# Delta-rule layer: decay exponentials in one piece behind the first keys' Silus, the keys' inverse square by reciprocal, powers of the queries behind the solve

## The chip, the cores and the metric

The kernel runs on one core of a Trainium2 chip. The metric is the device time of one execution in microseconds (us), given as the median of several runs. TensorE is called PE here, VectorE DVE, ScalarE ACT, GpSimd POOL and SyncE SP.

## What is computed

The program is a decoder trunk of four layers over 256 tokens of width 1024: a pooling mixer, a gated delta-rule mixer, a latent attention mixer, and a pooling mixer again. All of the change lies in the second layer, apart from one constant that an earlier layer sets up. Cut to what matters, that layer computes (8 heads, keys and queries of 128 channels, values of 256):

```
def l2norm(x):
    return x * rsqrt(sum(x * x, -1) + EPS)

qkv, gate, b_raw, a_raw = split(h @ w_in)
q, k, v = split(silu(causal_depthwise_conv(qkv, conv_w)))     # 4 taps
q = l2norm(q) * 128 ** -0.5;  k = l2norm(k)
beta = sigmoid(b_raw)
g = -exp(a_log) * softplus(a_raw + dt_bias)
# per chunk of tokens and head:
g = cumsum(g);  decay[i, j] = exp(g[i] - g[j]) for j <= i, else 0
L = strict_lower((k * beta) @ k.T * decay)
u, w = solve(I + L, [v * beta, k * beta * exp(g)])
attn = (q @ k.T) * decay
v_new = u - w @ state
o = (q * exp(g)) @ state + attn @ v_new
state = state * exp(g_last) + (k * exp(g_last - g)).T @ v_new
o = rmsnorm(o) * silu(gate);  y = o @ w_out
```

## The kernel before

**Strips.** Each weight matrix is read in strips of 512 columns. A strip comes in four DMAs on SP's queue, of two blocks of 128 rows each, into one of three raw buffers. Each block is split in two parts (`weights`, L126): ACT casts the high part (`whi`, L149), DVE (or POOL for a few blocks) subtracts it to get the low part (`wlo`, L150), and three matmuls make up one product (`mm3`). The split parts lie in a ring of nine. A gate strip (`g0` to `g3`) has tokens in the rows of its result; strips of keys, queries and values (`k`, `q`, `v`) have channels there.

**The layer's steps.** Behind the strip of a `k` or `q` step, `channels` (L791) does this: ACT scales the strip's PSUM results by the first tap (`conv`, L755), DVE adds the three other taps (L758), ACT takes the Silu (L804), PE transposes (L810), ACT squares the transposed block (L813), and DVE sums the squares into `ssq` (L814). For keys, ACT also copies the transposed first half into `ktok` (L816). `keys` (L838) makes the factors of the heads of one half: `rk`, the inverse root of the sum, as a power on POOL (L789), and `s2 = rk * beta * rk` on DVE. `lower` (L848) has PE multiply keys with keys (`against`, L818) and DVE multiply that by `s2` and by the decays `DT` into `LT` (L832); the diagonal blocks are copied out by POOL (L858) and ACT (L856).

**The solve.** `substitution` (L860) transposes the blocks on DVE (L861) and solves them by 62 small multiplications and subtractions on POOL, one after another (L867, L871). `blocks_back` (L876) transposes the result back on DVE (L878) and copies it into `T`, half on ACT (L885) and half on POOL (L887). `inverses` (L943) joins the blocks by matmuls between the next strips. `queries` (L893) multiplies keys with queries, and sets the powers `rq` and `rq2` of the queries' sums on POOL (L904, L789, L907, L908), which only the layer's last steps read. `ktok` is multiplied by a decay on POOL (L888); the steps of the state read it (`state`, L1027).

**Decays.** The cumulative sums `G` come from a small matmul; they go through DRAM and come back spread over all partitions as `Gb` (L733). DVE subtracts and masks (`DT`, L740, 16 instructions), and `decays` (L745) exponentiates both `DT`, `Gb[1]` and `G` itself (`eG`) on ACT (L748). Silu and Exp use different tables of ACT; a switch shows in the trace as ACT_TABLE_LOAD under the line of the next activation.

**What sets the order.** The steps are emitted in the order of a list written by hand:

```
order = "g0 k0 d a0 k1 a1 s g1 q0 v0 v1 v2 b q1 i V3 c3 g2 u0 u1 g3".split()
```

Here `a` is `lower`, `d` the decays, `s` the substitution, `b` `blocks_back`, `i` the inverses, and `u` the news of the values. The framework gets the program with `schedule_with_timeline_sim=True` (L1422): it fixes at build time, by a timeline of its own, in which order each engine executes what was emitted, and may take a later instruction first when an earlier one isn't ready on that timeline. In the trace, for instance, PE runs the whole strip of `k1` before the transposes of `k0`. On the chip each engine then works through its queue in that fixed order, and an instruction that waits holds up all behind it. `later(x)` (L82) forces the instructions emitted under it to come after instruction `x` on the engine of `x`; `mark` keeps the last instruction of several kinds: `mark["conv"]` the last tap, `mark["gate"]` the last Silu of a gate strip, `mark["blocks"]` the last step of the substitution, `mark["strip"]` the last matmul of a strip with channels in the rows.

Of the kernel before, what the change touches and what calls it, by code (L numbers as in the profile page):

```python
# [16 lines left out]
P = 128  # L17
# [7 lines left out]
EPS = 1e-6  # L25
# [17 lines left out]
def trunk(ctx: ExitStack, tc: tile.TileContext, x, positions, norm_g, pool_w_in, pool_w_grp,  # L43
# [466 lines left out]
    def pool_layer(i, j, hT):  # L510
# [80 lines left out]
        for g in order:  # L591
            gs = gate(g)
            if not place:
                with later(*[m for k, m in mark.items() if k not in ("rest", "strip", "conv")]):
                    turn_params()
                    window_counts()
            elif setups:
                with later(*[m for k, m in mark.items() if k not in ("rest", "strip", "conv")]):
                    setups.pop(0)()
            pT = pooled(g)  # L600
            if waiting:
                mixed(*waiting)
            waiting = (g, pT, gs)
# [8 lines left out]
    def gdn_setup():  # L612
# [11 lines left out]
        for a in range(2):  # L624
            nc.gpsimd.memset(m32[64 * a + 32:64 * a + 64, a], 1.0)
        half = const.tile([P, NT, GDN_H // 2], F32, name="halves")
        nc.gpsimd.memset(half, -0.5)
        cols = workb("cols", 2, 32)
# [28 lines left out]
    def gdn_layer(i, j, hT):  # L657
# [22 lines left out]

        order = "g0 k0 d a0 k1 a1 s g1 q0 v0 v1 v2 b q1 i V3 c3 g2 u0 u1 g3".split()
        while order[0][0] == "g":
# [38 lines left out]
        nc.vector.tensor_copy(flat(G), ps[:, :M])  # L721
        Gf, lf = flat(G), flat(lga)


# [12 lines left out]
        DT = [big("DT", H, P) for _ in range(NT)]  # L737
        for t in range(NT):
            for h in range(H):
                nc.vector.scalar_tensor_tensor(out=DT[t][:, h, :], in0=Gb[t][:, h, :],  # L740
                                               scalar=G[:, t, h:h + 1], in1=maskT,
                                               op0=ALU.subtract, op1=ALU.min)
        Eb = Gb[1]

        def decays():  # L745
            with later(*[m for n, m in mark.items() if n == "gate"]):
                for a in (*DT, Eb, eG):
                    nc.scalar.activation(a, G if a is eG else a, AF.Exp)  # L748

# [28 lines left out]
        for t in range(NT):  # L778
# [4 lines left out]
        ssq = small("ssq", 2, NT, H, bufs=1)  # L783
        rk, rki, rq, rq2, s1, s2 = (
            sc(n) for n in ("rk", "rki", "rq", "rq2", "s1", "s2"))
        neG = small("neG", H, bufs=1)

        def power(o, a):
            nc.gpsimd.tensor_tensor(out=o, in0=a, in1=half, op=ALU.pow)  # L789

        def channels(dst, c0, hf, which):  # L791
# [4 lines left out]
            for b in range(2):  # L796
                cv = [worka("cv", S) for _ in range(2)]
                conv(*[(banks[b][:, c * S:(c + 1) * S], (c0 + hf * CW) // P + 2 * b + c, cv[c])
                       for c in range(2)])
                for c in range(2):  # L800
                    o, v = dst[hf][:, 2 * b + c, :], cv[c]
                    if which:
                        o, v = halves(o), parted(v)
                    nc.scalar.activation(o, v, AF.Silu)  # L804
            for c in range(0, 4, 2):
# [32 lines left out]
        def keys(hf):  # L838
            hs = slice(4 * hf, 4 * hf + 4)
            channels(kT, GDN_QK, hf, 0)  # L840
            nc.gpsimd.tensor_scalar(ssq[:, 0, :, hs], ssq[:, 0, :, hs], EPS, None, ALU.add)
            power(rk[:, :, hs], ssq[:, 0, :, hs])
            nc.vector.tensor_tensor(out=s1[:, :, hs], in0=rk[:, :, hs], in1=beta[:, :, hs],
                                    op=ALU.mult)
            nc.vector.tensor_tensor(out=s2[:, :, hs], in0=s1[:, :, hs], in1=rk[:, :, hs],
                                    op=ALU.mult)

# [12 lines left out]
        def substitution():  # L860
# [3 lines left out]
            for r in range(B - 1):  # L864
# [7 lines left out]
                                                         op=ALU.subtract).ins  # L872
            nc.vector.reciprocal(rki, rk)
            nc.vector.tensor_scalar(neG, eG[:, 1, :], -1.0, None, ALU.mult)

        def blocks_back():  # L876
# [4 lines left out]
            for d in range(Q):  # L881
# [4 lines left out]
                else:  # L886
                    nc.gpsimd.tensor_copy(o, tv[dd])  # L887
            nc.gpsimd.tensor_tensor(out=ktok, in0=ktok, op=ALU.mult,  # L888
                                    in1=DT[0][:, :, P - 1:].to_broadcast([P, H, P]))

        at_ = []

        def queries(hf):  # L893
# [5 lines left out]
            ev = Eb[:, 4 * hf:4 * hf + 4, :]  # L899
            rh, qh = rq[:, :, 4 * hf:4 * hf + 4], rq2[:, :, 4 * hf:4 * hf + 4]  # L900

            nc.vector.tensor_tensor(out=ev, in0=ev, in1=qT[hf][:, :, P:], op=ALU.mult)
            with later(mark["blocks"]):
                nc.gpsimd.tensor_scalar(qh, ssq[:, 1, :, 4 * hf:4 * hf + 4], float(P), EPS * P,  # L904
                                        ALU.mult, ALU.add)
                power(rh, qh)
                nc.gpsimd.tensor_tensor(out=qh, in0=rh, in1=rh, op=ALU.mult)  # L907
                nc.gpsimd.tensor_scalar(qh, qh, 1.0 / DV, None, ALU.mult)  # L908

# [84 lines left out]
        def news(hf):  # L994
# [3 lines left out]
            for b in range(2):  # L998
# [6 lines left out]
                for c in range(2):  # L1005
# [5 lines left out]
                 "c": values_done}  # L1011
        once = {"s": substitution, "d": decays, "b": blocks_back, "i": inverses}
        for name in order:
# [419 lines left out]
```

## Time and profile before

| what | value |
|---|---|
| median of 3 runs | 816.21 us (813.97 to 816.85) |
| profiled execution | 817.07 us |
| its span, first to last instruction | 815.4 us |
| granted PE clock, mean | 0.992 |
| busy: PE, DVE, ACT, POOL | 794.6, 598.6, 500.2, 148.7 us |
| HBM read | 136.74 MB |

Rows of a timeline give the start, the duration, the engine, the line, the operation, output<-inputs, and how many instructions were merged; brackets hold the idle time of the engine ahead of the row and what ended it. Rows of a window give its bounds and length, the busy time of PE, PE's weight loads, DVE, ACT and POOL, the granted clock, and the DMA's share and rate. Matmul ends are modelled, so a busy PE says only that it had work. In this execution the delta-rule layer's strips run from about 170 to 340 us of the span.

### The profile page before, as it was taken

The numbers are of one execution on the slowest core, as the hardware profiler recorded it, in microseconds if no ns is written. First come the engines' busy times: TensorE is split into PE (matmuls) and PEld (weight loads), VectorE is DVE, ScalarE is ACT, GpSimd is POOL, SyncE is SP. The second block draws the span as 40 slices with busy tenths as digits, with TensorE's granted clock in tenths as the row PEclk, the third lists the DMA queues.
The fourth block names the chain that finished last, engine by engine and source line by source line (L and its number), as shares of the span: only waits on it lengthen the run. The fifth ranks groups of instructions, "written<-read, shape, count | busy, mean of one in ns | idle before, by whom it ended". The sixth has DMA issues, their size and how long they took to land.

```text
span 815.4 us, 16122 instructions
## 1 busy us (share of the span) xinstructions
PE 794.6 (97%) x5966; PEld 754.8 (93%) x5966; DVE 598.6 (73%) x1133; ACT 500.2 (61%) x1009; POOL 148.7 (18%) x292
## 2 busy tenths in 40 slices
PE   8989999999989989999999999999999999999996
PEld 7979999989889988888989999999999989999996
DVE  4699987667889976456677659778877667877863
ACT  6566555567876855455565654566655575566662
POOL 3001100233037852022212013000000210000011
PEclk9999999999999999999999999999999999999999
DMA  6765666746455633323557686753652646676562
GB/s 208 227 177 177 197 214 219 219 154 209 152 161 156 205 113 100 127 73 108 182 148 221 204 191 183 208 145 87 182 172 74 187 153 196 191 222 207 198 213 53
DMA packets 106615, 138.85 MB, mean 170 GB/s; under 512 B 19044, under 2 KB 48936, under 8 KB 106536
## 3 DMA queue, kind: packets, MB, share of 16 engines
q1 hardware_dynamic: 104032, 136.07, 55.2%
q0 software_dynamic: 320, 1.06, 0.4%
q8 instruction: 47, 0.77, 0.4%
q10 hardware_dynamic: 2184, 0.69, 0.4%
q14 instruction: 32, 0.26, 0.1%
HBM read 136.74 MB, written 1.06 MB: 169 GB/s over the span
## 4 chain that ended last, share of the span: by engine, by line
PE 85%; POOL 5%; ACT 3%; DVE 3%; issue 2%; DMA 1%; ACTq 0%; SPq 0%; DVEq 0%; POOLq 0%
PE acc L162 69%; PE aux L162 8%; POOL X L867 2%; POOL U L871 2%; ACT whi L149 1%; PE tp L1337 1%; DVE cv L758 1%; DMA x<-in_x_dram 1%; DVE wlo L150 1%; PE aux L823 1%; ACT junk L256 1%; PE tp L419 0%; PE aux L979 0%; PE aux L961 0%; PE aux L1002 0%
## 5 line engine op out<-in xcount | busy, mean ns | idle before, releaser
L150 DVE TENSOR_TENSOR wlo<-raw,whi 128x512 fp32r<-128x512 f32 (+1 forms) x370 | 250.1, 702 | 98.4 <-ACT whi L149 96.1
L149 ACT CAST whi<-raw 128x512 fp32r<-128x512 f32 (+1 forms) x380 | 223.1, 618 | 156.1 <-PE acc L162 78.9
L162 PE MATMUL acc<-hTl,whi 128*128 128x256 f32 x832 | 230.5, 277 | 0.0
L162 PE MATMUL acc<-hTh,whi 128*128 128x256 f32 x832 | 229.3, 276 | 0.0
L162 PE MATMUL acc<-hTh,wlo 128*128 128x256 f32 x832 | 229.1, 276 | 0.0
L162 PEld LDWEIGHTS acc<-hTl,whi 128*128 128x128 f32 x832 | 160.1, 192 | 0.2
L162 PEld LDWEIGHTS acc<-hTh,whi 128*128 128x128 f32 x832 | 160.0, 192 | 0.3
L162 PEld LDWEIGHTS acc<-hTh,wlo 128*128 128x128 f32 x832 | 159.9, 192 | 0.1
L162 PE MATMUL acc<-wlo,yTh 128*128 128x256 f32 (+1 forms) x384 | 112.3, 311 | 0.0
L162 PE MATMUL acc<-whi,yTh 128*128 128x256 f32 (+1 forms) x384 | 112.3, 315 | 0.0
L162 PE MATMUL acc<-whi,yTl 128*128 128x256 f32 (+1 forms) x384 | 89.1, 313 | 0.0
L162 PEld LDWEIGHTS acc<-wlo,yTh 128*128 128x128 f32 x384 | 73.2, 191 | 3.1
L162 PEld LDWEIGHTS acc<-whi,yTh 128*128 128x128 f32 x384 | 72.9, 191 | 3.1
L162 PEld LDWEIGHTS acc<-whi,yTl 128*128 128x128 f32 x384 | 63.1, 191 | 3.4
L153 ACT ACTIVATE whi<-raw,gain 128x512 fp32r<-128x512 f32 x64 | 43.7, 719 | 31.1 <-DMA raw<-in_pool_w_in_dram 25.6
L153 ACT ACTIVATE whi<-raw,colsT 128x512 fp32r<-128x512 f32 x64 | 44.5, 722 | 29.5 <-DMA raw<-in_pool_w_out_dram 18.1
L154 DVE SCALAR_TENSOR_TENSOR wlo<-raw,colsT,whi 128x512 fp32r<-128x512 f32 x64 | 47.4, 762 | 19.0 <-ACT whi L153 18.4
L162 PE MATMUL acc<-wlo,hTh 128*128 128x512 f32 (+1 forms) x144 | 54.1, 381 | 0.4 <-DVE wlo L150 0.2
L154 DVE SCALAR_TENSOR_TENSOR wlo<-raw,gain,whi 128x512 fp32r<-128x512 f32 x64 | 46.2, 743 | 10.0 <-ACT whi L153 7.5
L162 PE MATMUL acc<-whi,hTh 128*128 128x512 f32 (+1 forms) x144 | 52.8, 379 | 0.7 <-ACT hTh L242 0.7
L387 POOL TENSOR_TENSOR hg<-x,gain 128x256 f32<-128x256 f32 x16 | 13.4, 846 | 208.3 <-DVE x L451 208.3
L162 PE MATMUL acc<-whi,hTl 128*128 128x512 f32 (+1 forms) x144 | 42.5, 373 | 0.0
(368 smaller groups left out, 1526.2 us busy)
## 6 DMA issues: line engine op xcount, KB each, us to landing
raw<-in_pool_w_in_dram SPq DMA_DIRECT2D x62, 512.0 KB, 4.6
raw<-in_gdn_w_in_dram SPq DMA_DIRECT2D x48, 512.0 KB, 3.9
raw<-in_pool_w_out_dram SPq DMA_DIRECT2D x32, 512.0 KB, 4.6
raw<-in_mla_w_in_dram SPq DMA_DIRECT2D x24, 512.0 KB, 4.5
raw<-in_mla_w_uq_dram SPq DMA_DIRECT2D x36, 256.0 KB, 3.6
raw<-in_pool_w_grp_dram SPq DMA_DIRECT2D x16, 512.0 KB, 3.8
raw<-in_gdn_w_out_dram SPq DMA_DIRECT2D x16, 512.0 KB, 3.5
raw<-in_mla_w_ukv_dram SPq DMA_DIRECT2D x32, 256.0 KB, 3.4
```

The lines of the kernel that those rows point to most:

```text
L149: a = nc.scalar.copy(hi, v)
L150: b = e.tensor_tensor(out=lo, in0=v, in1=hi.bitcast(F32), op=ALU.subtract)
L153: a = nc.scalar.activation(hi, v, AF.Copy, scale=g)
L154: b = e.scalar_tensor_tensor(out=lo, in0=v, scalar=g, in1=hi.bitcast(F32), op0=ALU.mult, op1=ALU.subtract)
L162: return nc.tensor.matmul(inorder(o, n), lhsT=lhs, rhs=woven(rhs, n), start=start, stop=stop)
L256: nc.scalar.activation(junk[:, :n], src, AF.Square, scale=scale, accum_out=o)
L387: nc.gpsimd.tensor_tensor(out=self.early[t, a], in0=xs[t][:, sl], in1=self.g[:, sl], op=ALU.mult)
L758: mark["conv"] = nc.vector.scalar_tensor_tensor(out=o[:, d:], in0=ps[:, :S - d], scalar=tp(3 - d, c), in1=o[:, d:], op0=ALU.mult, op1=ALU. ...
L823: nc.tensor.matmul(ps[:, b], lhsT=kT[hf][:, b, tt], rhs=rhs[hf][:, b, tt], start=True, stop=True)
L867: nc.gpsimd.tensor_tensor(out=pv, op=ALU.mult, in0=Lb[:, r + 1:, r:r + 1].to_broadcast([P, n, c]), in1=Tb[:, r:r + 1, :c].to_broadcast([P, ...
L871: mark["blocks"] = nc.gpsimd.tensor_tensor(out=tv, in0=tv, in1=pv, op=ALU.subtract).ins
L1337: nc.tensor.transpose(ps[:, a * P:(a + 1) * P], sb[:, a * P:(a + 1) * P], ident)
```

## The change

Five things in the one layer:

1. `decays` no longer waits for the gate's Silu. It now holds the 16 subtractions of DVE too, and everything in it comes after the first keys' last tap on DVE (`mark["conv"]`) and after their last Silu on ACT (`mark["silu"]`, which is new). The exponential of `G` is emitted where `G` is made.
2. The keys' factor is `s2 = beta / (ssq + EPS)`, by a reciprocal and a multiplication on DVE. `rki`, which was the reciprocal of `rk`, is now the root of the sum, as a power of 0.5 on POOL.
3. The queries' powers leave `queries` for a step of their own, `query_norms` (`n`), behind `i`. Its instructions on POOL come after the last POOL copy of `blocks_back`.
4. The multiplication of `ktok` by the decay moves to the end of that step.
5. The list of steps has `q0` ahead of `g1`, and `n` behind `i`.

```
-        half = const.tile([P, NT, GDN_H // 2], F32, name="halves")
-        nc.gpsimd.memset(half, -0.5)
+        half = const.tile([P, 2, NT, GDN_H // 2], F32, name="halves")
+        for a in range(2):
+            nc.gpsimd.memset(half[:, a], a - 0.5)
...
-        order = "g0 k0 d a0 k1 a1 s g1 q0 v0 v1 v2 b q1 i V3 c3 g2 u0 u1 g3".split()
+        order = "g0 k0 d a0 k1 a1 s q0 g1 v0 v1 v2 b q1 i n V3 c3 g2 u0 u1 g3".split()
...
-        Gf, lf = flat(G), flat(lga)
+        Gf = flat(G)
+        nc.scalar.activation(eG, G, AF.Exp)
...
-        for t in range(NT):
-            for h in range(H):
-                nc.vector.scalar_tensor_tensor(out=DT[t][:, h, :], in0=Gb[t][:, h, :],
-                                               scalar=G[:, t, h:h + 1], in1=maskT,
-                                               op0=ALU.subtract, op1=ALU.min)
...
         def decays():
-            with later(*[m for n, m in mark.items() if n == "gate"]):
-                for a in (*DT, Eb, eG):
-                    nc.scalar.activation(a, G if a is eG else a, AF.Exp)
+            with later(mark["conv"], mark["silu"]):
+                for t in range(NT):
+                    for h in range(H):
+                        nc.vector.scalar_tensor_tensor(out=DT[t][:, h, :], in0=Gb[t][:, h, :],
+                                                       scalar=G[:, t, h:h + 1], in1=maskT,
+                                                       op0=ALU.subtract, op1=ALU.min)
+                for a in (*DT, Eb):
+                    nc.scalar.activation(a, a, AF.Exp)
...
-                    nc.scalar.activation(o, v, AF.Silu)
+                    mark["silu"] = nc.scalar.activation(o, v, AF.Silu).ins
...
-            nc.gpsimd.tensor_scalar(ssq[:, 0, :, hs], ssq[:, 0, :, hs], EPS, None, ALU.add)
-            power(rk[:, :, hs], ssq[:, 0, :, hs])
-            nc.vector.tensor_tensor(out=s1[:, :, hs], in0=rk[:, :, hs], in1=beta[:, :, hs],
-                                    op=ALU.mult)
-            nc.vector.tensor_tensor(out=s2[:, :, hs], in0=s1[:, :, hs], in1=rk[:, :, hs],
-                                    op=ALU.mult)
+            n, r = ssq[:, 0, :, hs], s2[:, :, hs]
+            nc.vector.tensor_scalar(n, n, EPS, None, ALU.add)
+            nc.vector.reciprocal(r, n)
+            nc.vector.tensor_tensor(out=r, in0=r, in1=beta[:, :, hs], op=ALU.mult)
+            nc.gpsimd.tensor_tensor(out=rki[:, :, hs], in0=n, in1=half[:, 1], op=ALU.pow)
...
-            nc.vector.reciprocal(rki, rk)
...
-                    nc.gpsimd.tensor_copy(o, tv[dd])
-            nc.gpsimd.tensor_tensor(out=ktok, in0=ktok, op=ALU.mult,
-                                    in1=DT[0][:, :, P - 1:].to_broadcast([P, H, P]))
+                    mark["back"] = nc.gpsimd.tensor_copy(o, tv[dd]).ins
...
-            with later(mark["blocks"]):
-                nc.gpsimd.tensor_scalar(qh, ssq[:, 1, :, 4 * hf:4 * hf + 4], float(P), EPS * P,
-                                        ALU.mult, ALU.add)
-                power(rh, qh)
-                nc.gpsimd.tensor_tensor(out=qh, in0=rh, in1=rh, op=ALU.mult)
-                nc.gpsimd.tensor_scalar(qh, qh, 1.0 / DV, None, ALU.mult)
+
+        def query_norms():
+            with later(mark["back"]):
+                nc.gpsimd.tensor_scalar(rq2, ssq[:, 1], float(P), EPS * P, ALU.mult, ALU.add)
+                for hf in range(2):
+                    hs = slice(4 * hf, 4 * hf + 4)
+                    nc.gpsimd.tensor_tensor(out=rq[:, :, hs], in0=rq2[:, :, hs], in1=half[:, 0],
+                                            op=ALU.pow)
+                nc.gpsimd.tensor_tensor(out=rq2, in0=rq, in1=rq, op=ALU.mult)
+                nc.gpsimd.tensor_scalar(rq2, rq2, 1.0 / DV, None, ALU.mult)
+                nc.gpsimd.tensor_tensor(out=ktok, in0=ktok, op=ALU.mult,
+                                        in1=DT[0][:, :, P - 1:].to_broadcast([P, H, P]))
...
-        once = {"s": substitution, "d": decays, "b": blocks_back, "i": inverses}
+        once = {"s": substitution, "d": decays, "b": blocks_back, "i": inverses,
+                "n": query_norms}
```

More of the change, by code (lines that the diff above doesn't have):

```diff
@@ L593, in pool_layer @@
             if not place:
-                with later(*[m for k, m in mark.items() if k not in ("rest", "strip", "conv")]):
+                with later(*[m for k, m in mark.items() if k not in ("rest", "strip", "conv", "silu")]):
                     turn_params()
@@ L597, in pool_layer @@
             elif setups:
-                with later(*[m for k, m in mark.items() if k not in ("rest", "strip", "conv")]):
+                with later(*[m for k, m in mark.items() if k not in ("rest", "strip", "conv", "silu")]):
                     setups.pop(0)()
@@ L783, in gdn_layer @@
         ssq = small("ssq", 2, NT, H, bufs=1)
-        rk, rki, rq, rq2, s1, s2 = (
-            sc(n) for n in ("rk", "rki", "rq", "rq2", "s1", "s2"))
+        rki, rq, rq2, s2 = (sc(n) for n in ("rki", "rq", "rq2", "s2"))
         neG = small("neG", H, bufs=1)
-        def power(o, a):
-            nc.gpsimd.tensor_tensor(out=o, in0=a, in1=half, op=ALU.pow)
         def channels(dst, c0, hf, which):
@@ L899, in queries @@
             ev = Eb[:, 4 * hf:4 * hf + 4, :]
-            rh, qh = rq[:, :, 4 * hf:4 * hf + 4], rq2[:, :, 4 * hf:4 * hf + 4]
             nc.vector.tensor_tensor(out=ev, in0=ev, in1=qT[hf][:, :, P:], op=ALU.mult)
-            with later(mark["blocks"]):
-                nc.gpsimd.tensor_scalar(qh, ssq[:, 1, :, 4 * hf:4 * hf + 4], float(P), EPS * P,
-                                        ALU.mult, ALU.add)
-                power(rh, qh)
-                nc.gpsimd.tensor_tensor(out=qh, in0=rh, in1=rh, op=ALU.mult)
-                nc.gpsimd.tensor_scalar(qh, qh, 1.0 / DV, None, ALU.mult)
+        def query_norms():
[9 more added lines that the diff above has]
+                                        in1=DT[0][:, :, P - 1:].to_broadcast([P, H, P]))
         vR = []
```

## The prediction

> **What bounds the kernel now.** I read the page's busy shares and its chain first, then the table of 5 us windows over the delta-rule layer, then the timelines of PE, ACT, DVE and POOL around each place where PE stood.
>
> ```profile
> span 815.4 us, 16122 instructions
> PE 794.6 (97%) x5966; PEld 754.8 (93%) x5966; DVE 598.6 (73%) x1133; ACT 500.2 (61%) x1009; POOL 148.7 (18%) x292
> PE 85%; POOL 5%; ACT 3%; DVE 3%; issue 2%; DMA 1%; ACTq 0%; SPq 0%; DVEq 0%; POOLq 0%
> ```
>
> PE is the bound: only 815.4 - 794.6 = 20.8 us of the span has no matmul running. The edit takes no matmul away, so it can gain only where PE waits, or where the clock drops behind a wait. The second thing to see is POOL's 5% of the chain with 18% of busy time: it is the substitution. The windows (start:end, length, busy PE, PEld, DVE, ACT, POOL, granted clock, DMA share, GB/s) show where PE lost time in this layer:
>
> ```profile
> 205.00:210.00 5.00, 3.74 (x25) 3.26 (x24) 5.00 (x16) 4.94 (x7) 0.00 (x0) 1.00 0.36 140
> 215.00:220.00 5.00, 5.00 (x34) 4.62 (x33) 4.58 (x10) 4.69 (x11) 1.93 (x2) 1.00 0.01 2
> 225.00:230.00 5.00, 1.65 (x10) 1.46 (x9) 4.29 (x12) 4.31 (x9) 1.91 (x4) 0.85 0.73 209
> 230.00:235.00 5.00, 5.00 (x39) 5.00 (x37) 2.92 (x5) 3.80 (x10) 1.62 (x1) 0.81 0.67 209
> 290.00:295.00 5.00, 2.37 (x22) 2.18 (x21) 4.32 (x10) 4.98 (x10) 4.60 (x7) 1.00 0.35 107
> 295.00:300.00 5.00, 5.00 (x34) 5.00 (x33) 4.96 (x8) 2.99 (x8) 0.75 (x1) 0.68 0.39 109
> ```
>
> PE's timeline names the three waits, all for a Silu (L804) that a strip's transposes (L810) read:
>
> ```profile
> 209.84 0.44 PE L810 MATMUL tp<-ident,kqT 128*128 128x128 f32 x2 [1.26 <-ACT kqT L804]
> 224.95 0.28 PE L162 MATMUL acc<-hTh,whi 128*128 128x256 f32 x1
> 228.58 0.69 PE L810 MATMUL tp<-ident,kqT 128*128 128x128 f32 x2 [3.35 <-ACT kqT L804]
> 294.78 0.44 PE L810 MATMUL tp<-ident,kqT 128*128 128x128 f32 x2 [2.63 <-ACT kqT L804]
> ```
>
> They belong to k0, k1 and q1. Behind the second and third the clock falls: (1 - 0.85) x 5 + (1 - 0.81) x 5 = 1.7 us lost, and (1 - 0.68) x 5 = 1.6. The first, 1.26 us, left it at 1.00. So 1.26 + 3.35 + 1.7 + 2.63 + 1.6 = 10.5 us is the most that this layer can give back. [...]
>
> **Why PE waited for k0 and k1.** ACT's queue:
>
> ```profile
> 192.19 0.21 ACT L748 ACTIVATE eG<-G 128x16 f32<-128x16 f32 x1
> 202.86 1.28 ACT L804 ACT_TABLE_LOAD   x1
> 204.15 1.03 ACT L804 ACTIVATE kqT<-cv 128x256 f32<-128x256 f32 x3
> 205.20 1.28 ACT L748 ACT_TABLE_LOAD   x1
> 208.08 1.28 ACT L804 ACT_TABLE_LOAD   x1
> 209.37 0.42 ACT L804 ACTIVATE kqT<-cv 128x256 f32<-128x256 f32 x1
> 210.83 1.28 ACT L748 ACT_TABLE_LOAD   x1
> 215.51 1.60 ACT L755 ACTIVATE cv<-acc,tap 128x256 f32<-128x256 f32 x4
> 216.94 2.74 ACT L149 CAST whi<-raw 128x512 fp32r<-128x512 f32 x5
> 222.98 1.15 ACT L149 CAST whi<-raw 128x512 fp32r<-128x512 f32 x2 [3.29 <-DMA raw<-in_gdn_w_in_dram]
> 226.81 1.28 ACT L804 ACT_TABLE_LOAD   x1
> ```
>
> Three Silus, an exponential behind the load at 205.20, the fourth Silu, the other exponentials behind the load at 210.83, and k1's Silus behind the one at 226.81: five loads, where three would do. k1's four scaled copies (215.51) and five weight casts come late, behind all of that. The casts free the raw buffers, so the weight DMAs stand still (2 GB/s in 215:220) and ACT next waits 3.29 us for weights.
>
> **The change, part by part.**
>
> *Exponentials in one piece.* They must now follow k0's last Silu, DVE's subtractions k0's last tap. Silu, Exp, Silu are three loads instead of five: 2 x 1.28 = 2.57 us leaves ACT's queue. [...] The subtractions are not made later: they wait for the broadcast anyway. The fourth Silu needs only the last tap, which stood behind them:
>
> ```profile
> 203.81 2.19 DVE L740 SCALAR_TENSOR_TENSOR DT<-Gb,G,maskT 128x128 f32<-128x128 f32 x8 [1.83 <-DMA Gb<-d_g]
> 205.92 0.47 DVE L758 SCALAR_TENSOR_TENSOR cv<-acc,tap,cv 128x253 f32<-128x253 f32 x1
> ```
>
> That tap fits into the 1.83 us, the Silu follows the third at about 205.2 + 0.4, and PE's first wait goes: 1.26 (bounds 0 and 1.26). The three exponentials come behind the Silus now; their first reader is k0's products (L832), which also need the keys' sums and are no input of k1's strip, so I count nothing for that. For k1, PE comes to the transposes at 224.95 + 0.28 - 1.26 = 224.0; the Silus, at 226.81 + 1.28 = 228.1 before, are due 2.57 earlier, 225.5. That leaves a wait of about 1.5, near the one of 1.26 that kept the clock, so I count 3.35 - 1.5 + 1.7 = 3.5 (bounds 0 and 5.05).
>
> *eG's exponential right behind G.* It ran there already (192.19): nothing, and if the planner moves it, one load of 1.28 more or less on ACT, where PE has the strip of k1 in hand.
>
> *Reciprocal for the keys.* Rows of k1:
>
> ```profile
> 232.24 1.45 DVE L814 TENSOR_REDUCE ssq<-sq 128x4 f32<-128x512 f32 x2 [1.05 <-ACT sq L813]
> 233.38 1.92 POOL L888 TENSOR_TENSOR ktok<-ktok,DT 128x1024 f32<-128x1024 f32 x1 [5.56 <-issue]
> 236.04 2.04 POOL L789 TENSOR_TENSOR rk<-ssq,halves 128x8 f32<-128x8 f32 x1
> 238.11 0.17 DVE L843 TENSOR_TENSOR s<-rk,beta 128x8 f32<-128x8 f32 x1 [0.77 <-POOL rk L789]
> 241.14 2.15 DVE L832 SCALAR_TENSOR_TENSOR LT<-aux,s,DT 128x128 f32<-128x128 f32 x8
> 246.57 2.06 DVE L861 STREAM_TRANSPOSE U<-X 128x1024 f32<-128x1024 f32 x1
> 288.84 1.07 DVE L878 STREAM_TRANSPOSE U<-U 128x512 f32<-128x512 f32 x1 [3.85 <-POOL U L871]
> ```
>
> From the sums' end (233.7) to the products (241.1) pass 7.4 us, through two POOL steps and two multiplications. Then come three DVE instructions of 8 columns: at about 0.2 each (the multiplication L843 is 0.17) 0.6 us if nothing stands between, 7.4 if the queue fills it; I take 2.4, a tap and two weight splits between, so 5.0 us gained. The square root for rki stays a power on POOL (2.04) beside the products; its only reader is the values' scaling (L934), three strips later, which is its cover. The sums themselves come about 3 us earlier with k1's transposes, and 1.7 by the clock: the substitution starts and ends 9.7 earlier in all (bounds 3 and 12).
>
> *The end of the substitution.* DVE stood 3.85 us at L878, with q1's taps behind it; so PE stood 2.63. PE now arrives 1.26 + 3.5 = 4.8 earlier, and q1's Silu may be 9.7 earlier: the wait goes if that is over 4.8 + 2.63 = 7.4. It does by 2.3: 2.63 + 1.6 = 4.2 gained (bounds: nothing, or all). What is late next is DVE itself.
>
> *Queries' powers and ktok behind the solve.*
>
> ```profile
> 289.17 1.65 POOL L789 TENSOR_TENSOR rq<-rq,halves 128x8 f32<-128x8 f32 x1
> 291.83 2.16 POOL L887 COPY T<-U 32x512 f32<-32x512 f32 x2
> 307.71 0.20 POOL L904 TENSOR_SCALAR rq<-ssq 128x8 f32<-128x8 f32 x1 [4.11 <-DVE ssq L814]
> L1029 PE MATMUL aux<-u,ktok x16: 379/379/382, 341.8 to 359.5; 128*128 128x256 f32 x16
> ```
>
> The copies of T no longer stand behind 3 us of q0's norms; that is on the way to the inverses, which fill PE between strips, and I count nothing for it. ktok's 1.92 goes to the end of a POOL queue that waits for q1's sums (307.7 before): 3 x 0.2 for the plain steps, 2 x 1.65 for the powers and 1.9 are 6 us, done by 314; its reader is at 341.8, cover 28 us. Behind that wait on POOL stand g2's weight splits (one in four of g2's), which the ring covers for some strips' worth: nothing, or up to one wait of 1.26. No DMA moves; one constant more is set in the first layer, where POOL idles.
>
> *q0 ahead of g1.* Same work for PE. But k0, k1 and q0 are now three strips in a row with taps on DVE, where the gate had none:
>
> ```profile
> 216.41 2.17 DVE L758 SCALAR_TENSOR_TENSOR cv<-acc,tap,cv 128x255 f32<-128x255 f32 x5 [0.32 <-ACT cv L755]
> L150 DVE TENSOR_TENSOR wlo<-raw,whi 128x512 fp32r<-128x512 f32 (+1 forms) x370 | 250.1, 702 | 98.4 <-ACT whi L149 96.1
> ```
>
> Twelve taps at 2.17 / 5 = 0.43 are 5.2 us of DVE, about 10 us sooner, beside DT and the products. New PE waits cost between 0 and one like k1's, 3.35 + 1.7 = 5.05; nearest are the small waits (1.26), and q0 transposes in two halves, so I take 2 x 1.26 = 2.5.
>
> **Sum.** 1.26 + 3.5 + 4.2 - 2.5 = 6.5 us. The profiled execution took 817.07 (span 815.4 and 1.7 around it), so 810.6; the median of the runs, 816.21, stands 0.86 lower, and I forecast 809.7.
>
> **Rivals.** (1) *The wait for k1 stays*: ACT keeps its Silus behind casts that wait for weights (the 3.29). For it: the planner fixes the order before it can know that wait; against it: the raw buffers come free 2.6 sooner. Then the gain is 1.26 + 4.2 - 2.5 = 3.0: 813.2. (2) *The exponentials are not in one piece*: the order binds only k0's Silus, k1's may fall between. Against it: k1's taps were 9 us later than the first exponential. Then the first wait may stay too: 4.2 - 2.5 = 1.7, 814.5. (3) *Slower: the solve starts later.* Once PE waits for nothing before it, the third wait is set by the substitution alone, and the whole change is the shift of its end. If DVE's queue has q0's taps (5.2), a pair of q0's sums (1.45) and g1's eight splits (8 x 250.1 / 370 = 5.4) ahead of k1's products and of L861, 12.1 us stand against what the keys gain: 9.7 by my terms, 2.4 later; but 1.26 + 5.0 = 6.3 where the wait for k1 stays as in (1), 5.8 later: 822.0. It decides for slower from 4.1 us later on. For it: three strips with taps in a row, and DVE at 4.96 to 5.00 in windows beside the strips. Against it: the keys' steps stand ahead of q0 in the program, and the substitution's transpose was only 3.3 us behind the products before.
>
> **How the numbers follow.** The forecast has 0.58, the rivals 0.20, 0.07 and 0.15. About 0.5% (4.1 us) is what a measurement of this kernel can tell from no change: faster is under 812.1, slower over 820.3. The forecast's own spread is 805 (10.5 and a little, no new waits) to 812; the first rival reaches under 812.1 with 0.02. So 0.60 faster, 0.26 the same, 0.14 slower. The range 805 to 819 leaves out the third rival and 0.05 below.
>
> **What would show it.** Right: three table loads between 202 and 230; no PE wait at k0's transposes and under 1.5 us at k1's, clock 1.00 there; the products within 3 us of the sums; the substitution from about 239 to 279; no wait at L878. Wrong: a new PE wait over 2 us for q0's Silus, DVE at 5.00 in every window from 205 to 240, or a substitution that starts after 246.

## The result, and the profile after

The changed kernel took 812.03 us (median of 8 runs, 811.54 to 812.91) beside 815.99 for the kernel before on the same chip (8 runs, 813.97 to 817.62): a ratio of 0.9947, 95% interval 0.993 to 0.9964. On another chip later it was 812.26 beside 818.09, a ratio of 0.9931 (0.9909 to 0.9952). The change makes the kernel faster, by 4.0 and 5.8 us by the medians; both intervals end below 1. The profiled execution took 811.58 with a span of 809.9, 5.5 below that of before. The page of the changed kernel:

```profile
span 809.9 us, 16112 instructions
PE 791.7 (98%) x5966; PEld 751.7 (93%) x5966; DVE 600.4 (74%) x1134; ACT 499.2 (62%) x1007; POOL 148.5 (18%) x288
PE 84%; POOL 5%; DMA 4%; DVE 3%; issue 2%; ACT 1%; SPq 0%; DVEq 0%; ACTq 0%
```

To read where 5.5 us came from, take the layer as one window, from the last addition of the first layer (DVE L451) to the last one of the second. First the kernel before, then the one after (columns as in the windows of the prediction):

```profile
166.42:409.03 242.61, 234.82 (x1703) 219.66 (x1702) 175.25 (x357) 156.90 (x331) 87.61 (x148) 0.99 0.47 146
```

```profile
165.94:403.56 237.62, 232.09 (x1703) 216.53 (x1702) 176.47 (x357) 153.93 (x329) 87.21 (x143) 1.00 0.47 149
```

5.0 of the 5.5 lie in this window; the other 0.5 is the first layer's end, 166.42 against 165.94, which no part of the change touches apart from a constant. So half a microsecond of every shift below that compares places in the two spans belongs to the first layer. In the layer PE's idle time (length less busy) fell from 7.8 to 5.5, and its busy time, for the same 1,703 matmuls, fell by 2.7. The clock is the likely reason: over 5 us slices of this window, 1 less the granted clock, times the slice, adds up to 3.4 us before and to nothing after. So 2.25 of idle time and 2.7 of busy time were gained; the clock lost 3.4 by that sum, and why the busy time fell by 0.7 less isn't shown.

**In this pair of executions over half of the gain is busy time, in step with a clock that no longer drops; the kernels' other executions show less.** The profiled execution of the changed kernel had the highest granted clock of its eight, 0.999 over the span, where their mean is 0.9952; and 811.58, 811.54 and 811.57 us were measured at 0.999, 0.996 and 0.993. On the second chip the mean is 0.9958 (9 executions) beside 0.9939 for the kernel before (16): 0.0019 of 815 us, 1.5 of the 5.8 gained there (an estimate; by the three times just given, not all of a lost clock is lost time).

The windows that were shown of before:

```profile
205.00:210.00 5.00, 5.00 (x47) 5.00 (x47) 5.00 (x16) 4.97 (x10) 0.00 (x0) 1.00 0.28 106
215.00:220.00 5.00, 5.00 (x32) 4.54 (x31) 5.00 (x12) 1.78 (x4) 1.28 (x1) 1.00 0.61 163
225.00:230.00 5.00, 5.00 (x31) 4.55 (x30) 4.45 (x12) 5.00 (x13) 1.64 (x1) 1.00 0.57 192
230.00:235.00 5.00, 5.00 (x47) 5.00 (x46) 5.00 (x15) 3.18 (x8) 1.14 (x4) 1.00 0.06 7
290.00:295.00 5.00, 4.35 (x37) 4.16 (x37) 4.46 (x10) 0.75 (x2) 0.00 (x0) 1.00 0.60 180
295.00:300.00 5.00, 3.97 (x40) 3.97 (x40) 3.77 (x7) 3.92 (x9) 1.28 (x1) 1.00 0.48 154
```

The windows shown between 205 and 235 are full of matmuls now; those from 290 to 300 are not. PE's timeline has these waits, the first for a Silu of q0, the others of q1 (L801 is the Silu's line now):

```profile
241.87 0.44 PE L807 MATMUL tp<-ident,kqT 128*128 128x128 f32 x2 [1.59 <-ACT kqT L801]
290.29 0.44 PE L807 MATMUL tp<-ident,kqT 128*128 128x128 f32 x2 [2.05 <-ACT kqT L801]
296.03 0.44 PE L807 MATMUL tp<-ident,kqT 128*128 128x128 f32 x2 [1.39 <-ACT kqT L801]
```

k0 and k1 wait no more. ACT's and DVE's timelines show why (a Silu load at 197.02 is the first of three loads):

```profile
205.99 1.28 ACT L749 ACT_TABLE_LOAD   x1
219.98 1.28 ACT L801 ACT_TABLE_LOAD   x1
221.27 0.72 ACT L801 ACTIVATE kqT<-cv 128x256 f32<-128x256 f32 x2
226.64 1.27 DVE L811 TENSOR_REDUCE ssq<-sq 128x4 f32<-128x512 f32 x2
227.94 0.17 DVE L839 TENSOR_SCALAR ssq<-ssq 128x8 f32<-128x8 f32 x1
228.60 0.19 DVE L840 RECIPROCAL s<-ssq 128x8 f32<-128x8 f32 x1
229.12 0.15 DVE L841 TENSOR_TENSOR s<-s,beta 128x8 f32<-128x8 f32 x1
230.36 2.16 DVE L829 SCALAR_TENSOR_TENSOR LT<-aux,s,DT 128x128 f32<-128x128 f32 x8
237.00 2.04 DVE L857 STREAM_TRANSPOSE U<-X 128x1024 f32<-128x1024 f32 x1
```

From the sums' end (227.9) to the products (230.36) it is 2.4 us instead of 7.4, and the products stand 10.8 earlier than before.

**What is left at q1.** DVE, ACT and POOL of the changed kernel around the end of the solve, one after the other:

```profile
279.05 1.08 DVE L873 STREAM_TRANSPOSE U<-U 128x512 f32<-128x512 f32 x1 [1.87 <-POOL U L867]
283.03 2.27 DVE L150 TENSOR_TENSOR wlo<-raw,whi 128x512 fp32r<-128x512 f32 x1 [2.33 <-ACT whi L149]
285.22 0.47 DVE L759 SCALAR_TENSOR_TENSOR cv<-acc,tap,cv 128x255 f32<-128x255 f32 x1
286.61 2.35 DVE L949 STREAM_TRANSPOSE U<-T 128x1024 f32<-128x1024 f32 x2
280.16 2.19 ACT L880 COPY T<-U 32x512 f32<-32x512 f32 x2 [2.10 <-DVE U L873]
282.90 0.83 ACT L756 ACTIVATE cv<-acc,tap 128x256 f32<-128x256 f32 x2
289.14 0.62 ACT L149 CAST whi<-raw 128x512 fp32r<-128x512 f32 x1 [1.89 <-DMA raw<-in_gdn_w_in_dram]
289.81 0.43 ACT L801 ACTIVATE kqT<-cv 128x256 f32<-128x256 f32 x1
295.02 0.62 ACT L149 CAST whi<-raw 128x512 fp32r<-128x512 f32 x1 [4.28 <-DMA raw<-in_gdn_w_in_dram]
282.83 1.92 POOL L904 TENSOR_TENSOR ktok<-ktok,DT 128x1024 f32<-128x1024 f32 x1
```

Read it as a chain. The last step of the solve ends on POOL; DVE transposes; ACT, which stood 2.10 us for that, copies T; only behind this copy come a cast and q1's first scaled copies (282.90); DVE stood 2.33 for that cast; its split of the weights, 0.69 in the median of the span, takes 2.27 while POOL multiplies ktok; then q1's taps start, with two transposes (2.35 together) among them. ACT then stands twice more for weights, 1.89 and 4.28 us, each time in a cast that its queue has just ahead of Silus of q1: late weights stand before those Silus too. In the kernel before, a pair of q1's scaled copies ran ahead of ACT's copy of T:

```profile
283.63 0.82 ACT L755 ACTIVATE cv<-acc,tap 128x256 f32<-128x256 f32 x2
289.94 2.21 ACT L885 COPY T<-U 32x512 f32<-32x512 f32 x2 [3.62 <-DVE U L878]
294.27 0.45 ACT L804 ACTIVATE kqT<-cv 128x256 f32<-128x256 f32 x1
```

From the transpose behind the solve to q1's first Silu it was 288.84 to 294.27, 5.4 us; now it is 279.05 to 289.81, 10.8 us. The solve came 9.8 us earlier, the Silu 4.5.

### The profile page after: what moved, and what is told of

It is laid out like the page before. It is cut to its first block, busy times and chain, and to the rows that moved or that the text cites. A ratio compares the mean times of both kernels' runs of the same rounds, so it can differ in the third digit from the quotient of the medians.

```text
span 809.9 us, 16112 instructions
## 1 busy us (share of the span) xinstructions
PE 791.7 (98%) x5966; PEld 751.7 (93%) x5966; DVE 600.4 (74%) x1134; ACT 499.2 (62%) x1007; POOL 148.5 (18%) x288
## 4 chain that ended last, share of the span: by engine, by line
PE 84%; POOL 5%; DMA 4%; DVE 3%; issue 2%; ACT 1%; SPq 0%; DVEq 0%; ACTq 0%
PE acc L162 68%; PE aux L162 8%; POOL X L863 2%; POOL U L867 2%; DMA raw<-in_pool_w_in_dram 2%; DVE wlo L150 1%; DMA x<-in_x_dram 1%; PE tp L1335 1%; PE aux L820 1%; DMA raw<-in_gdn_w_in_dram 1%; PE tp L419 0%; PE tp L1073 0%; PE aux L976 0%; DVE wlo L154 0%; PE aux L1036 0%
## 5 line engine op out<-in xcount | busy, mean ns | idle before, releaser
L162 PE MATMUL acc<-hTl,whi 128*128 128x256 f32 x832 | 230.5, 277 | 0.0
L162 PE MATMUL acc<-hTh,whi 128*128 128x256 f32 x832 | 229.2, 276 | 0.0
L162 PE MATMUL acc<-hTh,wlo 128*128 128x256 f32 x832 | 228.9, 275 | 0.0
L162 PEld LDWEIGHTS acc<-hTl,whi 128*128 128x128 f32 x832 | 159.8, 192 | 0.2
L162 PEld LDWEIGHTS acc<-hTh,whi 128*128 128x128 f32 x832 | 159.7, 192 | 0.3
L162 PEld LDWEIGHTS acc<-hTh,wlo 128*128 128x128 f32 x832 | 159.7, 192 | 0.1
L162 PE MATMUL acc<-wlo,yTh 128*128 128x256 f32 (+1 forms) x384 | 112.3, 311 | 0.0
L162 PE MATMUL acc<-whi,yTh 128*128 128x256 f32 (+1 forms) x384 | 112.3, 315 | 0.0
L162 PE MATMUL acc<-whi,yTl 128*128 128x256 f32 (+1 forms) x384 | 89.1, 313 | 0.0
L162 PEld LDWEIGHTS acc<-wlo,yTh 128*128 128x128 f32 x384 | 73.3, 191 | 3.1
L162 PEld LDWEIGHTS acc<-whi,yTh 128*128 128x128 f32 x384 | 72.9, 191 | 3.1
L162 PEld LDWEIGHTS acc<-whi,yTl 128*128 128x128 f32 x384 | 63.1, 191 | 3.4
L162 PE MATMUL acc<-wlo,hTh 128*128 128x512 f32 (+1 forms) x144 | 54.8, 386 | 0.4 <-DVE wlo L150 0.2
L162 PE MATMUL acc<-whi,hTh 128*128 128x512 f32 (+1 forms) x144 | 53.1, 380 | 0.7 <-ACT hTh L242 0.7
L162 PE MATMUL acc<-whi,hTl 128*128 128x512 f32 (+1 forms) x144 | 42.6, 374 | 0.0
```

What stands on the lines that cost most here:

```text
L162: return nc.tensor.matmul(inorder(o, n), lhsT=lhs, rhs=woven(rhs, n), start=start, stop=stop)
```

## The experiments

In the table, "layer" is the window above, "idle" PE's idle time in it, "clock" what the granted clock took (slices of 5 us), and "gap" the time from the transpose behind the solve to q1's first Silu. "Third" is the length of the third layer, by the same additions. Each row's layer, idle, clock, gap and third come from one execution, the profiled one; the ratio comes from all. Kernels e1 to e8 and f1 to f4 are each compared with the kernel before on their own chip.

| kernel | ratio (95%) | layer | idle | clock | gap | third |
|---|---|---|---|---|---|---|
| before | 1 | 242.6 | 7.8 | 3.4 | 5.4 | 247.05 |
| after | 0.9947 (0.993 to 0.9964) | 237.6 | 5.5 | 0 | 10.8 | 247.05 |
| e1 | 0.9979 (0.9958 to 1.0001) | 236.3 | 3.8 | 0 | 13.1 | 249.75 |
| e2 | 1.001 (0.9992 to 1.0029) | 244.6 | 8.7 | 3.4 | 13.3 | 247.12 |
| e3 | 0.999 (0.9972 to 1.0008) | 239.8 | 3.8 | 5.2 | 7.3 | 249.87 |
| e4 | 0.9947 (0.9928 to 0.9965) | 237.1 | 4.8 | 0 | 9.8 | 247.05 |
| e5 | 0.9912 (0.9881 to 0.9942) | 235.5 | 3.6 | 0 | 9.4 | 247.05 |
| e6 | 0.995 (0.9929 to 0.9972) | 235.2 | 4.3 | 0 | below 0 | 247.05 |
| e7 | 0.9916 (0.9882 to 0.9949) | 237.4 | 3.1 | 3.4 | below 0 | 247.05 |
| e8 | 1.0001 (0.9979 to 1.0023) | 241.2 | 6.3 | 3.4 | 12.0 | 247.05 |
| f1 | 0.9931 (0.9909 to 0.9952) | 237.5 | 5.4 | 0 | 10.7 | 247.05 |
| f2 | 0.9913 (0.9884 to 0.9942) | 235.0 | 3.2 | 0 | 9.4 | 247.05 |
| f3 | 0.9942 (0.992 to 0.9964) | 238.9 | 5.8 | 0 | 5.5 | 247.05 |
| f4 | 0.9887 (0.9861 to 0.9913) | 234.5 | 2.3 | 0 | 5.2 | 247.05 |

**e1_order_back**, the changed kernel with the gate strip ahead of q0 again:

```
-        order = "... s q0 g1 v0 v1 v2 b q1 i n V3 ..."
+        order = "... s g1 q0 v0 v1 v2 b q1 i n V3 ..."
```

> The changed kernel with the old order of the list (g1 ahead of q0), all else as changed. Theory A (the gain comes from ACT's table loads and from the shorter way of the keys; q0's early taps only cost): no PE wait at q0's transposes (1.59 us in the changed kernel), and the substitution starts earlier than 239 because q0's taps no longer stand ahead of its transpose on DVE, so q1's waits (2.05 + 1.39) shrink too: 809 us. Theory B (the order is what gives the gain, because a strip without waits stands between k1's strip and its transposes): PE waits for k1 again, some 3 us and the clock: 816 us.

Measured: theory A's waits, but not its 809 us. The layer is 1.4 us shorter than with the new order, q0 has no wait and q1's are 2.51 + 0.38 instead of 3.44; but the third layer, which the edit doesn't touch, is 2.7 longer. PE's timeline there (L419 and L162 at the end of that layer):

```profile
653.34 1.09 PE L419 MATMUL tp<-ident,h 128*128 128x128 f32 x8 [1.20 <-ACT h L404]
655.13 0.48 PE L162 MATMUL acc<-whi,hTh 128*128 128x512 f32 x1 [0.69 <-ACT hTh L242]
```

On DVE three of the four last additions to x (L451) run ahead of the first normalisation (L399), where the changed kernel has two ahead and two behind:

```profile
649.57 1.08 DVE L451 TENSOR_TENSOR x<-acc,x 128x256 f32<-128x256 f32 x3
652.78 0.88 DVE L399 SCALAR_TENSOR_TENSOR h<-x,xr,gain 128x256 f32<-128x256 f32 x2 [2.13 <-POOL xr L392]
```

So the order fixed at build time differs in a place 250 us behind the edited layer. In this trace the new place of q0 costs the layer 1.4; it pays here only because the old list, in the changed kernel, meets that other order in the third layer.

**e2_decays_back**, the changed kernel with `decays` as it was (the subtractions where `Gb` is made, the exponentials only behind the gate's Silu):

```
-            with later(mark["conv"], mark["silu"]):
-                ... (subtractions)
+            with later(mark["gate"]):
                 for a in (*DT, Eb):
```

> The changed kernel with the exponentials as before: subtractions right behind the broadcast, exponentials behind the gate's Silu only. Theory A (the loads between the Silus made PE wait for k0 and k1): five loads again, PE waits of about 1.3 at k0 and up to 3.4 at k1 with the clock's 1.7, the substitution some 3 us later: 815.5 us, 813 to 818. Theory B (the shorter way of the keys alone gives the gain): 812 us, within 1.

Measured: five table loads again, waits of 2.46 at k0, 0.98 at k1, 1.00 at q0, 1.03 at a values' strip and 2.60 at q1, with 3.4 of clock behind the last: the whole gain is gone, and the layer is 2.0 us longer than before. That is theory A, with more lost than it said. Here the split beside ktok took 1.89, and the gap is 13.3.

**e3_powers_back**, the changed kernel with the keys' factor as a power on POOL, the two multiplications and the reciprocal of `rk`:

```
-            nc.vector.reciprocal(r, n)
-            nc.vector.tensor_tensor(out=r, in0=r, in1=beta[:, :, hs], op=ALU.mult)
+            nc.gpsimd.tensor_tensor(out=rk[:, :, hs], in0=n, in1=half[:, 0], op=ALU.pow)
+            ... (s1 = rk * beta, s2 = s1 * rk on DVE)
```

> The changed kernel with the keys' factors by powers on POOL and rki by a reciprocal, as before. Theory A (q1's wait is set by the end of the substitution): the products start 7 instead of 2.5 us behind the sums, the substitution ends some 5 us later, q1's waits grow by as much, with the clock: 817 us. Theory B (q1's wait in the changed kernel is set by ACT, DVE and the weights behind ktok's multiplication, not by the substitution): q1's waits stay near 3.4, 812 to 813 us.

Measured: k0, k1 and q0 have no wait, but q1 waits 3.14 and the clock takes 5.2 more behind it; DVE stands 2.64 at the transpose behind the solve. The third layer is 2.8 longer, as in e1, so only the delta-rule layer is compared: 2.2 above the changed kernel. Theory A's 817 us was met by luck (817.59): q1's wait did not grow, as theory B said, and PE stands less in this layer than in the changed kernel, 3.8 against 5.5. The layer is longer by PE's busy time alone, behind the clock's 5.2, and the profiled execution had the lowest clock of the twelve (0.990; their mean is 0.9933). The ratio lies 0.0043 above that of the changed kernel, 3.5 us, which the third layer's 2.8 and 0.8 more in the fourth (153.1 against 152.3) would account for. So e3 doesn't show that the changed kernel needs the reciprocal.

**e4_queries_back**, the changed kernel with the queries' powers in `queries` and ktok's multiplication in `blocks_back`:

```
-        def query_norms(): ...
+            with later(mark["blocks"]):
+                ... (powers of one half, in queries)
+            ... (ktok *= DT, in blocks_back)
```

> The changed kernel with the queries' powers in the queries' step and ktok's multiplication in blocks_back, as before; n is gone from the list. Theory A (ktok's multiplication, moved to 282.8 beside a weight split that took 2.27 us there, delays q1's taps): that split takes 0.7 again, q1's waits shrink by 1.6: 810.5 us, though T's copies on POOL come 3 us later. Theory B (T's copies behind q0's powers are what counts at the inverses): PE waits later by up to 3 us more: 815 us.

Measured: the same ratio as the changed kernel, between the two theories. The split took 1.32, q1 waits 0.34 + 1.45, 1.65 less than in the changed kernel, but q0 waits 0.52 + 0.49 + 1.54. This part of the change as written brings nothing that these runs can tell.

**e5_ktok_last** and, once more on another chip, **f2_ktok_last**: the changed kernel with ktok behind the last of the powers on POOL.

```
-                nc.gpsimd.tensor_scalar(rq2, rq2, 1.0 / DV, None, ALU.mult)
+                last = nc.gpsimd.tensor_scalar(rq2, rq2, 1.0 / DV, None, ALU.mult).ins
+            with later(last):
                 nc.gpsimd.tensor_tensor(out=ktok, in0=ktok, op=ALU.mult,
```

> The changed kernel with ktok's multiplication ordered behind the last step of the queries' norms on POOL, some 20 us later. Theory A (ktok's multiplication holds up the weight split that took 2.27 us, and that delays q1's taps): the split takes 0.7, q1's waits fall from 3.44 to 1.8 us, the delta-rule layer (237.6 us from the last addition to x of the layer before it to its own last one) to 236: ratio 0.993. Theory B (the wait for weights, 4.28 us on ACT, sets q1's Silus, whatever the split takes): q1's waits stay near 3.4, ratio 0.995.

> ktok's multiplication behind the powers of the queries, once more. Theory A (its place in front of the solve's copies' readers cost PE 2.05 + 1.39 at the second and third of q1's... waits, of which 0.84 stayed): 1.5 to 2.2 us less than the changed kernel in the layer, ratio to before 0.991 to 0.993. Rival (the 0.9912 of the first run was the chip's): the ratio of the changed kernel, 0.9947 within 0.001.

Measured: 2.2 and 2.5 us less in the layer than the changed kernel (237.6 to 235.5, 237.5 to 235.0); q1 waits 0.84 (e5) and 1.20 (f2) instead of 3.44 (after) and 2.85 (f1). The times say it less surely: f2's ratio and f1's, 0.9913 and 0.9931 on one chip, have intervals that overlap, and the medians differ by 0.8 us. In f2, the split and the wait that stays:

```profile
282.18 0.69 DVE L150 TENSOR_TENSOR wlo<-raw,whi 128x512 fp32r<-128x512 f32 x1 [2.32 <-ACT whi L149]
292.74 0.62 ACT L149 CAST whi<-raw 128x512 fp32r<-128x512 f32 x1 [4.08 <-DMA raw<-in_gdn_w_in_dram]
293.74 0.44 PE L807 MATMUL tp<-ident,kqT 128*128 128x128 f32 x2 [1.20 <-ACT kqT L801]
```

The split is back to 0.69, where f1 on the same chip has 2.27; so in the traces the rival (a chip's chance) doesn't hold, while the times leave it open. e5's theory B is right in part: the wait that stays comes behind a cast for which ACT stood 4.08 us for weights. DVE's wait of 2.3 for the cast behind the copy of T stays too, and so does most of the gap.

**e6_b_behind_q1** and **e7_both**: the copies of the solve's result behind q1's strip, without and with e5's edit.

```
-        order = "... v2 b q1 i n V3 ..."
+        order = "... v2 q1 b i n V3 ..."
```

> The changed kernel with b behind q1 in the list: DVE takes q1's taps ahead of the transposes that wait for the substitution. Theory A (q1's wait comes from its taps standing behind the end of the substitution on DVE and ACT): q1's waits of 3.44 go, the layer falls to 234.2 us, ratio 0.9905. Theory B (the solve itself is the bound by then: what the transposes of q1 no longer wait for, the joining of the blocks waits for): a PE wait of 2 to 4 us at the inverses, ratio 0.994 to 0.996.

> b behind q1 and ktok's multiplication last. Theory A: as with b behind q1 alone, since q1's taps are then ahead of the substitution's end and of ktok anyway: layer 234.2 us, within 0.5 of that run. Theory B (ktok's multiplication blocks DVE wherever it runs beside weight splits): 1 to 1.6 us less than that run.

Measured: in e6 q1 has no wait, so it is the solve's result in the queues ahead of q1's copies, taps and Silus that held q1 up. The layer is 1.0 longer than theory A's 234.2: a values' strip waits 0.85 and the inverses' matmuls 0.79, less than theory B said. In e7 the inverses wait the same 0.79, and the clock fell in the slice of that wait and in the next:

```profile
331.50 1.97 PE L983 MATMUL aux<-U,X 64*64 64x64 f32 x16 [0.79 <-DVE X L980]
```

```profile
330.00:335.00 5.00, 4.21 (x27) 3.69 (x27) 2.00 (x4) 0.00 (x0) 0.00 (x0) 0.63 0.34 110
335.00:340.00 5.00, 5.00 (x18) 4.04 (x16) 0.11 (x1) 3.02 (x8) 0.00 (x0) 0.69 0.00 0
```

The two slices add up to 3.4 us of clock; if all of it was lost time, the layer would be 234.0 without the drop (an estimate, 237.4 - 3.4), so e7 decides between its theories no more than the times do. By the times neither is told apart from the changed kernel (e6) or from e5 (e7).

**e8_decays_only**: the kernel before with change 1 (the decays in one piece), and nothing else.

```
             with later(mark["conv"], mark["silu"]):
                 ... (subtractions, then exponentials)
```

> The kernel before with the exponentials in one piece alone: no reciprocal, the old order of the list, powers and ktok as before. Theory A (the waits at k0 and k1 come from the table loads, but what PE wins there it waits for again at q1, because the substitution ends only some 4 us earlier): no waits at k0 and k1, q1's wait 2.6 to 5 us; layer 238 to 239 against 242.6, ratio 0.995. Theory B (each part adds its own gain; the decays' share is the 1.3 us of the first wait and 1.3 of the second): layer 240, ratio 0.997.

Measured: no gain in the time, 1.4 us in the layer. It is theory A's account, with more given back than it said: k0 has no wait and k1 one of 0.39, but PE waits twice as long at q1:

```profile
294.50 0.69 PE L811 MATMUL tp<-ident,kqT 128*128 128x128 f32 x2 [5.38 <-ACT kqT L805]
```

**f3_reciprocal_only**: the kernel before with the keys' reciprocal alone, `rki` as a power of POOL, decays, order and queries as before.

```
-            power(rk[:, :, hs], ssq[:, 0, :, hs])
-            ... (s1, s2)
+            nc.vector.reciprocal(r, n)
+            nc.vector.tensor_tensor(out=r, in0=r, in1=beta[:, :, hs], op=ALU.mult)
+            nc.gpsimd.tensor_tensor(out=rki[:, :, hs], in0=n, in1=half[:, 1], op=ALU.pow)
```

> The kernel before with the keys' reciprocal alone (rki as a power, the rest as before, the decays and the list too). Theory S (PE's wait for q1 is set by the solve's end, and the two parts are not independent): the products come some 4 to 5 us earlier and with them the solve, q1's wait (2.63 and its clock loss of 1.6) goes, k0's 1.26 and k1's 3.35 stay; the layer 242.6 - 4.2 = 238.4, ratio 0.995. Rival (the keys' path was no part of the bound; the solve starts earlier and DVE comes late anyway): the wait for q1 stays over 2 us, the layer 241.5 to 242.6, ratio 0.999 to 1.

Measured: the layer 238.9 (theory S: 238.4), ratio 0.9942. q1's wait is 0.26 instead of 2.63; k0's stayed:

```profile
210.32 0.44 PE L811 MATMUL tp<-ident,kqT 128*128 128x128 f32 x2 [1.26 <-ACT kqT L805]
221.43 0.44 PE L811 MATMUL tp<-ident,kqT 128*128 128x128 f32 x2 [1.42 <-ACT kqT L805]
227.24 0.44 PE L811 MATMUL tp<-ident,kqT 128*128 128x128 f32 x2 [1.11 <-ACT kqT L805]
291.54 0.44 PE L811 MATMUL tp<-ident,kqT 128*128 128x128 f32 x2 [0.26 <-ACT kqT L805]
```

Not expected: k1's wait became two of 1.42 and 1.11 that left the clock alone, though there are five loads still: the last of them starts at 219.67 instead of 226.81, so the planner's order changed there too. That theory S hit the length is in part luck, since some of the gain is k1's. And the solve ends later than in the changed kernel, with q1's Silu only 5.5 behind it:

```profile
285.58 1.06 DVE L877 STREAM_TRANSPOSE U<-U 128x512 f32<-128x512 f32 x1 [1.49 <-POOL U L871]
291.04 0.45 ACT L805 ACTIVATE kqT<-cv 128x256 f32<-128x256 f32 x1
```

**By the times, the reciprocal alone can't be told from the whole change**: 0.9942 beside f1's 0.9931 on the same chip, intervals that overlap. In the layer it gains 3.7 us, the whole change 5.0.

**f1_after**, the changed kernel itself, and **f4_ktok_g1**, f2 with g1 behind v0:

```
-        order = "... s q0 g1 v0 v1 ..."
+        order = "... s q0 v0 g1 v1 ..."
```

> The changed kernel itself, beside the next three on one chip. Ratio to before 0.9947 as in the first comparison (0.993 to 0.996); the layer 237.6 us, from the last addition to x of the first layer to the last one of the second.

> ktok's multiplication last, and the gate strip g1 behind v0 instead of ahead of it: four strips with taps in a row (k1, q0, v0 with k0 before them). Theory B (taps in a row cost PE waits at q0, 1.59 to 2.2 so far, and the gate strip gives DVE its rest; with g1 ahead of q0 the layer was 1.4 shorter): the layer 1 to 3 us longer than with ktok last alone, 236.5 to 238.5, ratio 0.993 to 0.996. Rival (only the strip right behind k1 matters): the layer 235.5, ratio 0.991 to 0.992.

Measured: f1 as expected, its ratio at the lower end. f4 has the lowest median of all, 808.65 us (808.12 to 810.69) beside f1's 812.26 and 818.09 for the kernel before (its interval still overlaps f2's), and theory B falls: more strips with taps in a row did not lengthen the layer. PE's waits are 1.14 at k1 and 0.49 at q1. ACT's timeline shows the gap closed, since a pair of q1's scaled copies runs ahead of the copy of T again:

```profile
281.53 0.82 ACT L756 ACTIVATE cv<-acc,tap 128x256 f32<-128x256 f32 x2
282.38 2.18 ACT L880 COPY T<-U 32x512 f32<-32x512 f32 x2
285.99 0.43 ACT L801 ACTIVATE kqT<-cv 128x256 f32<-128x256 f32 x1
```

The kernels where such a pair stands ahead of the copy (before, f3, f4) have gaps of 5.2 to 5.5; those where all stand behind it (after, f1, f2, e1 to e5, e8) of 7.3 to 13.3. No run changes that place alone.

## Why the prediction was right, and where its sum was off

The direction held: 4.0 us gained where 6.5 were forecast, and 5.0 in the layer. It was a near thing: the median of 812.03 lies 0.07 under the 812.1 that the prediction drew as its line for faster, though the interval is clear of 1. The mechanism held part by part, each shown alone on the kernel before: the decays take away the waits at k0 and k1 but for 0.39 us (e8), the reciprocal the one at q1 but for 0.26 (f3). It failed where the parts meet, at q1.

- *First wait*: gone, 1.26 as forecast. The fourth Silu stands before the exponentials (e2: undone, k0 waits 2.46).
- *Second wait*: 3.5 forecast, 5.05 measured. The forecast left 1.5 of it; none stayed, and the clock kept 1.00. It was reckoned from k1's old place in ACT's queue less two loads, but the taps of k0 and k1 and the casts moved up too: k1's first Silu came 6.8 earlier (228.1 to 221.3), not 2.6.
- *The keys' path*: from the sums to the products 7.4 us became 2.4, as forecast; with five taps between them, not a tap and two splits. The substitution's transpose, 246.57 before, stands at 237.00: 9.6 earlier against 9.7. The closeness is luck in part: the sums came 5.8 earlier, not 4.7, and the transpose stands 6.6 behind the products, not 5.4. That the reciprocal can carry most of the gain is shown by f3; that the gain needs it isn't (e3).
- *Third wait*: **this step failed.** 4.2 forecast; 0.8 measured (2.63 of wait and 1.6 of clock became 2.05 + 1.39 of wait; 1.73 + 1.12 in f1). The step took q1's Silu to move with the solve's end, by 9.7. The end did move by 9.8, and PE came 3.9 earlier (292.15 to 288.24) instead of 4.8, which leaves a larger margin than was reckoned; but the Silu moved by 4.5 alone. "What is late next is DVE itself" named an engine that then stood 2.33 us for ACT: what held q1 up was ACT's queue, where the copy of T, which waits for the solve, now stands ahead of q1's copies, and behind them the casts that wait for weights. DVE's own wait at the transpose did not go either: 1.87 of 3.85 stayed.
- *ktok*: "goes to the end of a POOL queue that waits for q1's sums" was wrong. Nothing but the last copy of T binds it, so the planner put it right behind those copies, beside the split that q1's taps wait for; e5 and f2 price that at 2.2 and 2.5 us of the layer. The cover of 28 us at its reader was right, but the cost lay with a neighbour. The traces show it: a split beside ktok's multiplication took 2.27 us (after), 1.89 (e2), 1.68 (e1), 1.96 (f4) and 1.42 (e8), and 0.69 where ktok ran later (f2, at 282.18). In the changed kernel POOL began 0.20 us before the split, which ended 0.55 behind POOL; in e1, e8 and f4 it ended 0.54 to 0.55 behind too. In f2 it was the other way round: a split of 0.68 ran inside ktok's multiplication, which took 2.67 instead of 1.92. What ties the two together isn't shown.
- *New waits at q0*: 2.5 forecast, 1.59 measured (1.96 in f1). By e1's trace the new place of q0 costs 1.4 in the layer.
- *The sum*: 1.26 + 5.05 + 0.8 - 1.6 = 5.5 by waits and clock, 5.0 by the layer's length; the 0.5 between them stays unexplained. That 5.5 is near 6.5 is cancellation: the second wait gave 1.5 more and q0 cost 0.9 less than forecast, the third wait gave 3.4 less.
- *Rivals*: the first (k1's Silus behind late casts) did not come, although ACT waits 2.30 for weights just before them; the second neither: three loads. The third's condition came true in part: five of q0's taps stand on DVE ahead of k1's products, and four more with five weight splits between the products and the transpose. The transpose stands 1.2 us further behind the products than before (6.6, not 5.4), and the solve came earlier all the same.

The terms were added as if independent. They are not: the decays alone gain nothing that the time shows (e8, 1.0001), since what PE wins at k0 and k1 it waits for again at q1; with all other parts in, undoing the decays costs 7.0 us of the layer (e2, 244.6). With the reciprocal alone the old decays leave it at 238.9 (f3): so the new order and the queries' step pay only together with the decays. What no run tells apart is why the planner puts q1's copies ahead of the copy of T in one kernel and behind in the next.

## What to carry to other kernels

When a wait on a serial chain is shortened, follow the engine queue of each reader behind it: here the solve came 9.8 us earlier and the Silu behind it only 4.5, with ACT's copy of the solve's result, a split of 2.27 us and late weights ahead of it. An instruction that nobody waits for still needs a place; put it by an explicit order where it blocks no neighbour, because the planner here put it in the first place that the order allowed. After an edit that changes a planned order, compare also the layers that were not edited: 2.7 us went there in e1. And before a gain is put down to the clock, compare the granted clock of all executions, not of the two that were profiled.

## What the runs showed of the hardware

Whether the clock drops could not be told from the length of PE's wait. It fell at a wait of 0.79 us in e7 (0.63 and 0.69 in two slices of 5 us) and stayed at 1.00 at the same wait in e6; at waits of 2.60, 2.63, 3.35 and 5.38 it fell (e2, before, e8), at 1.26, 1.59, 2.05, 2.46 (k0 of e2) and 2.51 (e1) it did not. It differs between executions of one kernel too: over the span it was 0.992 to 0.999 in the eight of the changed kernel. Likewise e5 and f2 are the same program (0.996 and 0.998 over the span of the profiled executions), and in the first layer, where PE idles for over 2 us between 55 and 60, the clock of the slice from 60 to 65 is 0.70 in e5 and 1.00 in f2.

What the granted clock lost in the layer came in steps: 1.7 twice in before (the prediction's 1.6 is without the 0.1 of the slice from 300 to 305), 3.4 in e2, e7 and e8, 5.2 in e3, near to one, two and three times 1.7. Both drops of before are to 0.50 for 3.4 us, from 228.50 to 231.91 and from 296.78 to 300.18. The first begins where PE's wait ends (228.58), the second 2.0 us behind it (294.78). What sets the start and the length of a drop isn't shown. The loss shows in PE's busy time of the layer (length less idle), for 1,695 to 1,703 matmuls in the traces: 234.3 to 236.0 us in the five traces with a drop, 230.9 to 233.1 in the nine without.
